# Taking GpSimd off SBUF in the first part of a two-layer block: its arithmetic moved to VectorE

## The chip, the cores and the metric

The kernel runs on one core of one Trainium2 chip. The core's engines are TensorE (PE: matrix products and transposes, results in PSUM), VectorE (DVE), ScalarE (ACT), GpSimd (POOL) and SyncE (SP, which here only issues DMA transfers). Each engine works through its own queue of instructions in order and waits on semaphores for the others. The metric is the time of one execution on the device in microseconds (us), the median of several executions; one execution more was recorded with a profile, and all rows below come from that one.

## The reference, cut to what matters

Two blocks follow each other on 256 tokens of width 2048, all in float32. The first is an RWKV-7 block and a feed-forward network, both modulated by a vector computed from a condition `c` (the ada projection, 2048 x 12288); the second is an attention and convolution block with a gated projection.

```
mod = silu(c) @ ada_w + ada_b                       # six vectors of 2048
h = rms(x) * (1 + sc_m) + sh_m
xx = token_shift(h) - h
r, k, v = (h + xx * mu[i]) @ w_rkv[i]               # three mixes, and three more for the low ranks
w, a, g = low-rank functions of further mixes
y = rwkv7_scan(r, decay, k, v, -kk, kk * a)         # 32 heads of 64, a recurrence over tokens
x = x + g_m * rms((groupnorm(y) + bonus) * g @ w_o)
h = rms(x) * (1 + sc_f) + sh_f
x = x + g_f * rms((silu(gate) * val) @ w_out)       # gate, val = conv(h @ w_in), hidden 5504
x = second_block(x)                                 # attention, short conv, w_out, gated projection
```

## The kernel before

Each matrix product is done in three passes: an operand is split into a high part (rounded, by ScalarE) and a low part (the remainder, by a subtraction), and TensorE adds high x high, high x low and low x high. Activations and weights are both split. For weights this is the helper `split` (line 133): a unit of 128 x 1024 is loaded into `raw`, ScalarE writes `whi` (line 143), and line 147 writes `wlo = raw - whi`. Which engine does that subtraction is a running count: with `share[0]` = n every n-th unit goes to GpSimd and the others to VectorE; `n_pool[0]`, set at the begin of some stages, sends the next few units to GpSimd.

The stages in order of time, with the letters by which the text calls them:

- **A**, the mixes and the k, v and low-rank products, in five groups of the 16 row tiles (`GROUPS`). `prep` and `mix` (line 366) make the mixed activations: VectorE writes `mt` (line 373), ScalarE the high part (line 376), and line 377 the low part, on VectorE for one mix of six and on GpSimd for the others.
- **B**, a loop over 16 pairs of heads. For each pair the low-rank products, decay, keys and the r product (two weight units) are made; GpSimd splits the low-rank weights (line 563), copies the last decay of each chunk into `EC` (line 588), and does the two multiplications of lines 593 and 603.
- **C**, the chunked scan over four chunks of 64 tokens. At its start (called the head here) VectorE inverts 32 x 32 triangles by a long row of small operations (`invert_diag`, lines 682 and 685), while `gram` (line 687) makes the Gram matrices: TensorE writes them to PSUM, ScalarE copies them to SBUF (line 705), and GpSimd multiplies the mask in (line 706); 16 of these 32 multiplications belong to the head. After it, line 806 multiplies the state by the decay on GpSimd.
- **D**, the output projection `w_o`, with `share[0]` = 3.
- **E**, the residual (`add_residual`, line 983), the second norm and the transposes into the feed-forward layout (`to_fm`; line 1002 scales, line 1022 writes low parts, two of eight on GpSimd).
- **F**, everything behind: the feed-forward network and the second block.

Through B, C, D and E, and again through F, runs the accumulation of the ada projection (`ada_group`, line 223) as a generator: each step loads two tiles of `ada_w` into a ring of buffers (three from B on) and adds them into an accumulator. `ada_pool[0]` = 1 sends one row tile of four to ScalarE (line 243, into `nbr`) and GpSimd (line 244), the other three are one VectorE instruction each (line 246); `ada_fm` then adds the two accumulators on GpSimd (line 279) before TensorE sums them over partitions.

A scheduler places the instructions on each engine's queue when the program is built, from the written order and its dependencies, so the written order shows only which work belongs together. DMA transfers are all issued from SP's queue.

## Time and profile before

| | |
|---|---|
| median of 3 executions | 2203.3 us (2195.14 to 2216.86) |
| the profiled execution, on the device | 2202.33 us |
| its span, first to last instruction | 2200.5 us |
| mean granted TensorE clock | 0.938 of full speed |
| busy: PE / DVE / ACT / POOL | 2007.2 / 1390.0 / 1025.5 / 770.4 us |
| DMA | 445.26 MB, mean 202 GB/s |

Times in the rows are microseconds from the span's start. An engine counts as busy while any of its instructions stands in the record. A timeline row gives start, duration, engine, source line, operation, what it writes and reads with the shapes, how many were merged, and in brackets the idle time of the engine before it with what ended it. Two VectorE instructions without a dependency overlap in the record by some 0.06 to 0.1 us, so a row of n merged ones lasts a little less than n times one.

### The profile page before, as it was taken

The page shows a single profiled execution, that of the slowest core. Times are in us where ns is not written, and L with a number is a line of the kernel's source. Part 1 is how long each engine was busy: PE and PEld are TensorE (multiplying, and loading weights), DVE is VectorE, ACT ScalarE, POOL GpSimd, SP SyncE. Part 2 cuts the span into 40 slices and gives each one's busy share as a digit, 9 for nine tenths or more (in the row PEclk, how much of TensorE's full clock was granted, in tenths as well). Part 3 has the DMA queues.
Part 4 walks back from the last instruction along what each step waited for, and adds up shares of the span by engine and source line. Part 5 has one row for each costly group of instructions (what it writes and reads, how often), then busy time and mean ns, then how long its engine had stood idle before and what let it go on. Part 6 is the DMA issues. An engine that isn't in the chain of part 4 may idle for free.

```text
span 2200.5 us, 36863 instructions
## 1 busy us (share of the span) xinstructions
PE 2007.2 (91%) x14708; PEld 1752.7 (80%) x14708; DVE 1390.0 (63%) x1975; ACT 1025.5 (47%) x1594; POOL 770.4 (35%) x437
## 2 busy tenths in 40 slices
PE   6889988987799696899999999999998999999998
PEld 3578777876577475789989999878886799998887
DVE  3576998987877767786666675433335565656435
ACT  3434455553344434555545545444435454454443
POOL 2332445656145334343333232222322222222232
PEclk9999998999679698899999999999999999999999
DMA  8778567774566687676676565665554444456554
GB/s 293 252 249 301 180 207 240 241 230 96 140 160 182 224 288 261 219 270 197 197 215 203 193 209 191 196 214 189 188 190 145 147 158 163 160 163 209 186 194 152
DMA packets 189037, 445.26 MB, mean 202 GB/s; under 512 B 40121, under 2 KB 62777, under 8 KB 187329
## 3 DMA queue, kind: packets, MB, share of 16 engines
q1 hardware_dynamic: 188864, 442.91, 62.4%
q8 instruction: 115, 1.88, 0.3%
q14 instruction: 58, 0.47, 0.1%
HBM read 427.10 MB, written 15.75 MB: 201 GB/s over the span
## 4 chain that ended last, share of the span: by engine, by line
PE 51%; DVE 5%; DMA 4%; ACT 1%; issue 1%; POOL 1%; SPq 0%; ACTq 0%; POOLq 0%; DVEq 0%
PE ps_s L158 6%; PE ps_s L160 6%; PE ps_s L159 5%; PE ps_s L175 4%; PE ps_s L174 4%; PE ps_s L173 4%; PE ps_g L158 4%; PE ps_g L160 4%; PE ps_g L159 4%; PE ps_g L173 3%; PE ps_g L175 3%; PE ps_g L174 3%; DMA raw<-in_ada_w 2%; DVE acc L246 1%; DVE wlo L147 1%
## 5 line engine op out<-in xcount | busy, mean ns | idle before, releaser
L143 ACT ACTIVATE whi<-raw 128x1024 fp32r<-128x1024 f32 x558 | 588.5, 1057 | 647.7 <-PE ps_s L174 126.5
L147 POOL TENSOR_TENSOR wlo<-raw,whi 128x1024 fp32r<-128x1024 f32 x185 | 458.1, 2477 | 984.6 <-ACT whi L143 950.0
L147 DVE TENSOR_TENSOR wlo<-raw,whi 128x1024 fp32r<-128x1024 f32 x373 | 480.3, 1290 | 439.5 <-ACT whi L143 435.2
L160 PE MATMUL ps_g<-xh,wlo 128*128 128x256 f32 x816 | 235.5, 289 | 7.6 <-DVE wlo L147 7.0
L160 PE MATMUL ps_s<-xh,wlo 128*128 128x256 f32 x816 | 230.7, 283 | 9.6 <-DVE wlo L147 9.3
L159 PE MATMUL ps_g<-xl,whi 128*128 128x256 f32 x816 | 235.0, 288 | 2.5 <-POOL xl L1022 2.5
L158 PE MATMUL ps_g<-xh,whi 128*128 128x256 f32 x816 | 235.8, 289 | 0.7 <-DVE kac L407 0.6
L158 PE MATMUL ps_s<-xh,whi 128*128 128x256 f32 x816 | 230.1, 282 | 2.6 <-ACT whi L143 2.6
L159 PE MATMUL ps_s<-xl,whi 128*128 128x256 f32 x816 | 229.6, 281 | 0.0
L246 DVE SCALAR_TENSOR_TENSOR acc<-raw,sil,acc 128x512 f32<-128x512 f32 x176 | 184.5, 1048 | 28.0 <-DMA raw<-in_ada_w 26.6
L160 PEld LDWEIGHTS ps_g<-xh,wlo 128*128 128x128 f32 x816 | 160.5, 197 | 10.4 <-DVE wlo L147 9.6
L160 PEld LDWEIGHTS ps_s<-xh,wlo 128*128 128x128 f32 x816 | 156.5, 192 | 11.4 <-DVE wlo L147 10.7
L159 PEld LDWEIGHTS ps_g<-xl,whi 128*128 128x128 f32 x816 | 161.7, 198 | 4.7 <-POOL xl L1022 2.7
L158 PEld LDWEIGHTS ps_g<-xh,whi 128*128 128x128 f32 x816 | 160.9, 197 | 4.4 <-ACT whi L143 1.3
L158 PEld LDWEIGHTS ps_s<-xh,whi 128*128 128x128 f32 x816 | 156.7, 192 | 3.0 <-ACT whi L143 3.0
L159 PEld LDWEIGHTS ps_s<-xl,whi 128*128 128x128 f32 x816 | 157.3, 193 | 0.0
L244 POOL TENSOR_TENSOR acc<-acc,nbr 128x512 f32<-128x512 f32 x48 | 75.5, 1572 | 140.6 <-ACT nbr L243 139.7
L158 PE MATMUL ps_s<-h3h,whi 128*128 128x256 f32 x384 | 109.6, 285 | 0.0
L160 PE MATMUL ps_s<-h3h,wlo 128*128 128x256 f32 x384 | 108.8, 283 | 0.0
L159 PE MATMUL ps_s<-h3l,whi 128*128 128x256 f32 x384 | 108.4, 282 | 0.0
L373 DVE SCALAR_TENSOR_TENSOR mt<-xx,vec,h 128x256 f32<-128x256 f32 x96 | 75.5, 828 | 6.9 <-POOL yl L377 4.7
L158 PEld LDWEIGHTS ps_s<-h3h,whi 128*128 128x128 f32 x384 | 72.5, 189 | 3.6 <-issue 3.5
(519 smaller groups left out, 4981.7 us busy)
## 6 DMA issues: line engine op xcount, KB each, us to landing
raw<-in_w_f SPq DMA_DIRECT2D x258, 512.0 KB, 4.4
raw<-in_ada_w SPq DMA_DIRECT2D x192, 512.0 KB, 5.2
raw<-in_w_i2f SPq DMA_DIRECT2D x80, 512.0 KB, 3.7
raw<-in_w_o SPq DMA_DIRECT2D x60, 512.0 KB, 4.7
raw<-in_w_v SPq DMA_DIRECT2D x32, 512.0 KB, 4.0
raw<-in_w_k SPq DMA_DIRECT2D x32, 512.0 KB, 4.3
raw<-in_w_r SPq DMA_DIRECT2D x32, 512.0 KB, 6.7
raw<-in_w_g SPq DMA_DIRECT2D x32, 512.0 KB, 4.7
```

The source lines that it names most:

```text
L143: S.activation(hi, raw, AF.Copy)
L147: e.tensor_sub(lo, raw, hi)
L158: mm(acc, wh[:, sl], xh[:, kt, :], start=(kt == 0), stop=False)
L159: mm(acc, wh[:, sl], xl[:, kt, :], start=False, stop=False)
L160: mm(acc, wl[:, sl], xh[:, kt, :], start=False, stop=(kt == KT - 1))
L173: mm(a, xh, wh[:, sl], start=st, stop=False)
L174: mm(a, xl, wh[:, sl], start=False, stop=False)
L175: mm(a, xh, wl[:, sl], start=False, stop=sp_)
L244: G.tensor_tensor(acc, acc, tp, op=ALU.add)
L246: V.scalar_tensor_tensor(acc, raw[:, a, :], sc, acc, op0=ALU.mult, op1=ALU.add)
L373: V.scalar_tensor_tensor(mt[:, i, :], xx[:, k0 + i, :], vcol(V_MU, m * 16 + k0 + i), hx[:, k0 + i, :], op0=ALU.mult, op1=ALU.add)
```

## The change

From the first stretch (A) to the output projection and the residual (E), every instruction with which GpSimd read SBUF moves to VectorE; what GpSimd keeps there are memsets and the four additions of squares at the very start (line 359). In parts:

- `split`: the low parts of all weight units of A, B and D on VectorE (`SH`, and 9999 instead of 3 for the output projection). `share[0]` = 3 comes back before F.
- `mix`: the low part always on VectorE. `to_fm`: likewise (`TFP` goes).
- B: lines 563, 593 and 603 on VectorE; the copy into `EC` becomes a second, small exponential on ScalarE, read from the same sums.
- `gram`: one VectorE instruction reads PSUM and multiplies the mask, in place of ScalarE's copy and GpSimd's multiplication.
- The state's decay (line 806) on VectorE.
- `ada_pool` stays 0: all row tiles of the ada projection are added by VectorE, and lines 238, 243, 244 and 279 no longer run, in F too.

```
-SH = (4, 3)
+SH = (9999, 9999)
...
-        (V if m == 1 else G).tensor_sub(dst[1][:, ks, :], mt, dst[0][:, ks, :])
+        V.tensor_sub(dst[1][:, ks, :], mt, dst[0][:, ks, :])
...
     ada_how[0] = ada_group
-    ada_pool[0] = 1
...
-        G.tensor_sub(l2l, l2, l2h)
+        V.tensor_sub(l2l, l2, l2h)
...
-        G.tensor_copy(EC[:, j, :], ep[:, :, 64])
+        S.activation(EC[:, j, :], c3(pc)[:, :, 63], AF.Exp, scale=C1)
...
-        G.tensor_tensor(k2, k2, kr, op=ALU.mult)
+        V.tensor_tensor(k2, k2, kr, op=ALU.mult)
...
-        G.tensor_tensor(bk[:, :, 64:128], c3(k2), em, op=ALU.mult)
+        V.tensor_tensor(bk[:, :, 64:128], c3(k2), em, op=ALU.mult)
...
-                S.activation(gg, gp[hd].rearrange("p (c t) -> p c t", t=P), AF.Copy)
-                G.tensor_tensor(gg, gg, gmask[:, None, :].broadcast_to([P, 4, P]), op=ALU.mult)
+                V.tensor_tensor(gg, gp[hd].rearrange("p (c t) -> p c t", t=P),
+                                gmask[:, None, :].broadcast_to([P, 4, P]), op=ALU.mult)
...
-                        G.tensor_tensor(s_, s_, ec, op=ALU.mult)
+                        V.tensor_tensor(s_, s_, ec, op=ALU.mult)
...
-    n_raw[0], share[0] = NRAW2, 3
+    n_raw[0], share[0] = NRAW2, 9999
...
-                e = G if k2 % TFP == 2 else V
-                e.tensor_sub(dst[1][:, ks, :], tf, dst[0][:, ks, :])
+                V.tensor_sub(dst[1][:, ks, :], tf, dst[0][:, ks, :])
...
     pho.close()
 
+    share[0] = 3
     n_pool[0] = NPL
```

The scheduler's order changes with it. Line numbers behind line 33 are one to seven lower after the change. In the loop over head pairs (B), VectorE's queue for one pair stood before as follows, from the evaluation of one pair (`qb`, line 610) to the next:

```order
L610 SCALAR_TENSOR_TENSOR qb<-ps_g,vec,k_3575 128x256
L240 TENSOR_SCALAR acc_3814<-raw,sil 128x512
L620 TENSOR_TENSOR vT<-vT,ps_m 128x256
L623 SCALAR_TENSOR_TENSOR vT<-vT,vec,ps_s 128x256
L246 SCALAR_TENSOR_TENSOR acc_3814<-raw,sil,acc_3814 128x512
L597 SCALAR_TENSOR_TENSOR kn<-kr,vec,ps_m 128x256
L582 SCALAR_TENSOR_TENSOR pc<-smask,thw 128x256
L246 SCALAR_TENSOR_TENSOR acc_3814<-raw,sil,acc_3814 128x512
L599 SCALAR_TENSOR_TENSOR AR<-kn,ep 128x4x64
L601 SCALAR_TENSOR_TENSOR pc<-tha,em 128x256
L602 SCALAR_TENSOR_TENSOR BK<-pc,kn 128x4x64
L607 TENSOR_TENSOR AR<-ps_g,ep 128x4x64
```

After the change the second half of the same place, up to the next pair's evaluation, reads:

```order
L146 TENSOR_TENSOR wlo<-raw,whi 128x1024
L597 SCALAR_TENSOR_TENSOR AR<-kn,ep 128x4x64
L599 SCALAR_TENSOR_TENSOR pc<-tha,em 128x256
L601 TENSOR_TENSOR BK<-k_3705,em 128x4x64
L600 SCALAR_TENSOR_TENSOR BK<-pc,kn 128x4x64
L239 TENSOR_SCALAR acc_3805<-raw,sil 128x512
L561 TENSOR_TENSOR l2l<-l_3812,l2h 128x512
L245 SCALAR_TENSOR_TENSOR acc_3805<-raw,sil,acc_3805 128x512
L146 TENSOR_TENSOR wlo<-raw,whi 128x1024
L605 TENSOR_TENSOR AR<-ps_g,ep 128x4x64
L608 SCALAR_TENSOR_TENSOR qb<-ps_g,vec,k_3705 128x256
```

The multiplication into `BK` (601), the low-rank low part (561) and the weight units' low parts (146) now stand in VectorE's queue ahead of the evaluation for which TensorE waits.

At the scan's head VectorE's queue began before with the masked diagonal blocks (659), a transpose, and at once the row of small operations of the inversion (682, 685):

```order
L623 SCALAR_TENSOR_TENSOR vT<-vT,vec,ps_s 128x256
L659 TENSOR_TENSOR TQ<-ps_s,cst 128x16x32 x2
L662 STREAM_TRANSPOSE NT<-TQ 128x1024
L670 COPY XT<-NT 128x1024
L682 TENSOR_TENSOR pt_5220<-XT,NT 128x30
L682 TENSOR_TENSOR pt_5241<-XT,NT 128x23
```

After the change the masks of the Gram matrices (703, from PSUM) stand between them:

```order
L621 SCALAR_TENSOR_TENSOR vT<-vT,vec,ps_s 128x256
L703 TENSOR_TENSOR xh<-ps_m,cst 128x4x128
L657 TENSOR_TENSOR TQ<-ps_s,cst 128x16x32 x2
L703 TENSOR_TENSOR xh<-ps_a,cst 128x4x128
L660 STREAM_TRANSPOSE NT<-TQ 128x1024
L703 TENSOR_TENSOR xh<-ps_m,cst 128x4x128
L668 COPY XT<-NT 128x1024
L703 TENSOR_TENSOR xh<-ps_m,cst 128x4x128
L680 TENSOR_TENSOR pt_5197<-XT,NT 128x30
```

Four of the 16 masks of the head stand here and twelve near the end of the first inversion; all 16 come before the transpose (725 before, 723 after) for which TensorE waits.

In the residual (E), VectorE's queue before, from the first root to the scaling by the second (1002):

```order
L338 RECIPROCAL rsy<-rsy 128x1
L983 SCALAR_TENSOR_TENSOR xt<-y_8004,rsy,xt 128x512 x2
L1051 TENSOR_TENSOR y_8004<-ps_s,grow 128x512
L983 SCALAR_TENSOR_TENSOR xt<-y_8004,rsy,xt 128x512 x2
L246 SCALAR_TENSOR_TENSOR acc_8644<-raw,sil,acc_8644 128x512
L975 TENSOR_REDUCE rsy<-ssq 128x1
L246 SCALAR_TENSOR_TENSOR acc_8644<-raw,sil,acc_8644 128x512 x2
L338 RECIPROCAL rsy<-rsy 128x1
L246 SCALAR_TENSOR_TENSOR acc_8644<-raw,sil,acc_8644 128x512
L983 SCALAR_TENSOR_TENSOR xt<-y_8004,rsy,xt 128x512 x4
L975 TENSOR_REDUCE rsx<-ssq_8553 128x1
L246 SCALAR_TENSOR_TENSOR acc_8644<-raw,sil,acc_8644 128x512
```

And after:

```order
L337 RECIPROCAL rsy<-rsy 128x1
L977 SCALAR_TENSOR_TENSOR xt<-y_7898,rsy,xt 128x512 x2
L1044 TENSOR_TENSOR y_7898<-ps_s,grow 128x512
L977 SCALAR_TENSOR_TENSOR xt<-y_7898,rsy,xt 128x512 x2
L969 TENSOR_REDUCE rsy<-ssq 128x1
L337 RECIPROCAL rsy<-rsy 128x1
L977 SCALAR_TENSOR_TENSOR xt<-y_7898,rsy,xt 128x512 x4
L969 TENSOR_REDUCE rsx<-ssq_8434 128x1
L337 RECIPROCAL rsx<-rsx 128x1
L996 TENSOR_SCALAR y_7898<-xt,rsx 128x512 x3
```

Five additions of the ada projection (246) stood inside this piece of the queue; after the change they stand ahead of it.

## Rows read from the trace of the kernel before

**Rows 1.** The page: the span, and part 1, busy us, share, instructions.

```profile
span 2200.5 us, 36863 instructions
PE 2007.2 (91%) x14708; PEld 1752.7 (80%) x14708; DVE 1390.0 (63%) x1975; ACT 1025.5 (47%) x1594; POOL 770.4 (35%) x437
```

**Rows 2.** Busy us by stretch (A, B, head, C, D, E): PE, PEld, DVE, ACT, POOL; clock, DMA.

```profile
35.00:325.00 290.00, 260.97 (x1680) 206.30 (x1678) 209.60 (x254) 133.57 (x172) 101.28 (x44) 0.97 0.71 239
325.00:505.00 180.00, 160.47 (x1146) 146.23 (x1146) 154.34 (x208) 96.39 (x188) 107.17 (x106) 0.91 0.72 226
505.00:565.00 60.00, 34.74 (x654) 27.65 (x643) 48.07 (x129) 18.08 (x36) 35.31 (x21) 0.80 0.42 98
565.00:725.00 160.00, 151.41 (x2145) 121.82 (x2142) 122.54 (x255) 75.34 (x169) 63.48 (x51) 0.78 0.65 171
725.00:860.00 135.00, 110.14 (x474) 84.32 (x471) 93.85 (x109) 56.23 (x83) 53.94 (x27) 0.84 0.75 262
860.00:910.00 50.00, 27.75 (x170) 25.21 (x169) 38.27 (x59) 24.35 (x51) 18.69 (x10) 0.73 0.63 221
```

**Rows 3.** TensorE's waits, one stretch each (A, B, head, D, E, E): us, times, longest.

```profile
PE ps_s L426 <- POOL wlo L147: 4.3, 1, 4.3
...
PE ps_m L612 <- DVE qb L610: 10.4, 5, 2.6
...
PE ps_m L735 <- DVE TQ L725: 15.9, 1, 15.9
...
PE ps_g L175 <- POOL wlo L147: 2.4, 2, 1.8
...
PE ps_m L1006 <- DVE y L1002: 17.9, 2, 17.0
PE ps_g L159 <- POOL xl L1022: 2.5, 1, 2.5
```

**Rows 4.** Timeline: VectorE instructions beside which GpSimd reads nothing.

```profile
143.86 2.45 DVE L373 SCALAR_TENSOR_TENSOR mt<-xx,vec,h 128x256 f32<-128x256 f32 x6
824.92 1.23 DVE L147 TENSOR_TENSOR wlo<-raw,whi 128x1024 fp32r<-128x1024 f32 x1 [4.19 <-ACT whi L143]
837.29 0.75 DVE L246 SCALAR_TENSOR_TENSOR acc<-raw,sil,acc 128x512 f32<-128x512 f32 x1 [0.73 <-DMA raw<-in_ada_w]
```

**Rows 5.** VectorE's groups of instructions in A (first row) and B: busy us, mean ns.

```profile
L373 DVE SCALAR_TENSOR_TENSOR mt<-xx,vec,h 128x256 f32<-128x256 f32 x92 | 72.8, 832 | 6.8 <-POOL yl L377 4.7 <-POOL xl L377 1.8
...
L246 DVE SCALAR_TENSOR_TENSOR acc<-raw,sil,acc 128x512 f32<-128x512 f32 x33 | 37.5, 1138 | 0.9 <-DMA raw<-in_ada_w 0.8
...
L602 DVE SCALAR_TENSOR_TENSOR BK<-pc,kn 128x256 f32<-128x256 f32 x16 | 20.0, 1248 | 0.3
```

**Rows 6.** Timeline of the scan's head: VectorE's inversion, and GpSimd's masks beside it.

```profile
516.97 1.29 DVE L659 TENSOR_TENSOR TQ<-ps_s,cst 128x512 f32<-128x512 f32 x2 [11.79 <-PE ps_s L655]
...
537.49 2.57 DVE L685 TENSOR_TENSOR XT<-XT,pt 128x91 f32<-128x91 f32 x2
...
549.82 0.35 DVE L682 TENSOR_TENSOR pt<-XT,NT 128x70 f32<-128x70 f32 x2
...
556.89 1.38 DVE L682 TENSOR_TENSOR pt<-XT,NT 128x23 f32<-128x23 f32 x2
...
561.86 1.99 DVE L725 STREAM_TRANSPOSE TQ<-XT 32x1024 f32<-32x1024 f32 x1
...
525.54 18.12 POOL L706 TENSOR_TENSOR xh<-xh,cst 128x512 f32<-128x512 f32 x6
```

**Rows 7.** Timeline of E: VectorE.

```profile
866.08 4.23 DVE L983 SCALAR_TENSOR_TENSOR xt<-y,rsy,xt 128x512 f32<-128x512 f32 x2
...
873.76 3.51 DVE L246 SCALAR_TENSOR_TENSOR acc<-raw,sil,acc 128x512 f32<-128x512 f32 x2
...
881.54 4.06 DVE L1002 TENSOR_SCALAR y<-xt,rsx 128x512 f32<-128x512 f32 x2
...
885.59 0.87 DVE L1002 TENSOR_SCALAR y<-xt,rsx 128x512 f32<-128x512 f32 x2
```

More of the change, by code (lines that the diff above doesn't have):

```diff
@@ L33 @@
 OSTEP = (2, 2, 2, 0)
-TFP = 8
 RSKIP = (0, 4)
@@ L896, in ada_steps @@
     def ada_steps(n):
-        ada_pool[0] = 4
         for _ in range(n):
             next(ada, None)
-        ada_pool[0] = 1
         yield
@@ L905, in body @@
         run(HD[nm]())
-    ada_pool[0] = 1
     dg = invert_diag(1, PARTS)
@@ L958, in body @@
             y_split(yh[1][:, :, p4, (c - 2) * 64:(c - 1) * 64], YS[c][:, p4, :])
-    ada_pool[0] = 1
     phb.close()
```

## The prediction, made before the run

> **What bounds the kernel now.** I read the page first: TensorE is busy for 91% of a span of 2200.5 us, VectorE for 63%, GpSimd for 35% [rows 1]. Such shares average stages with different limits, so the next view is the busy time by stretch [rows 2]. Up to 910 us, where the change acts, TensorE has gaps: 290.0 - 261.0 = 29.0 us in A, 180.0 - 160.5 = 19.5 in B, 25.3 in the head of the scan, 8.6 in the rest of C, 24.9 in D and 22.3 in E, together 130 us. No change to the vector engines can give back more than that, apart from the clock (granted share 0.73 to 0.97 in these stretches). Behind 910 us GpSimd keeps its third of the weight units, and I count that part as unchanged.
>
> Then the waits of TensorE, stretch by stretch [rows 3]. In A one wait of 4.3 us is for a low part made by GpSimd. In B it is for `qb` on VectorE, in the head 15.9 us in one piece for VectorE's transpose behind the inversion, in D partly for GpSimd's low parts, in E 17.9 us for VectorE's scaling and 2.5 for a low part of GpSimd. So in B, the head and E the engine that is waited for is VectorE, the one that gets the work.
>
> The last view is what VectorE's instructions last. With GpSimd not reading, a low part of a weight unit (128x1024) takes 1.23 us, an ada addition 0.75, and six mixes of 128x256 together 2.45, or 0.41 each [rows 4]; two masked blocks of 128x512, read from PSUM as the Gram matrices will be, take 1.29 [rows 6]. Yet the 92 mixes of A have a mean of 0.83 us, the 33 ada additions of B 1.14, and the 16 of line 602 there 1.25 [rows 5]. In the scan's head it is seen directly: a pair of small operations takes 2.57 us at 537.49 and 0.35 at 549.82, and in the first of these places GpSimd is in a run of six masks, 18.12 us or 3.02 each [rows 6]. Two engines that never wait for each other's data slow each other by whole instructions. The Trainium skill, "SBUF — State Buffer", section "Who interferes with whom", states this as an exclusive lock: a VectorE instruction with two inputs in SBUF and a GpSimd instruction that reads SBUF exclude each other. The trace agrees, with 2.57 against 0.35 us.
>
> **The change part by part.** The moved work, at these durations, less the roughly 0.1 us by which independent neighbours overlap.
>
> *A.* VectorE gets 18 weight low parts at 1.13 (20 us), 13 mixes' low parts of 128x1024 at 1.13 (15) and 13 of 128x512 at about 0.62 (8): 43 us. The excess that should leave is 92 x (0.83 - 0.41) = 39 us in the mixes alone [rows 4, 5], some more in the weight units. VectorE stays near 210 of 290 us. TensorE's gain is in single waits: in the one of 4.3 us, GpSimd made two low parts one after the other; on VectorE they take 1.2 each, about 2 us sooner. Counting one more such place: -4. Bounds: -15, if half of A's 29 us of gaps go; +5, if low parts that had an engine of their own queue behind mixes.
>
> *B.* VectorE gets 10 weight low parts (11 us), 12 ada additions (8), 16 low-rank low parts of 128x512 at 0.6 (10) and 32 multiplications of 128x256 at 0.36 (11): 40 us. It loses 33 x (1.14 - 0.75) = 13 us in the ada additions, 16 x (1.25 - 0.42) = 13 in line 602, and some of the remaining groups. It is busy for 154 of 180 us now, and so it will be after. The order shows the moved work in front of the evaluation that TensorE waits for; before, the same place was delayed by blocked instructions of up to 2.5 us. I take -2. Bounds: -10.4, the wait on `qb`; +14, if nothing of the excess comes back: 154 + 40 = 194, against 180. The exponential that replaces the copy into `EC`, 128x4, lies on ScalarE, idle for 84 us of B: nothing; without that cover its 16 would cost below 0.4 us each.
>
> *The head of C.* From 516.97 to 561.86 VectorE runs without a gap, 44.9 us [rows 6], and TensorE waits for what comes at the end. From 537.49 to 549.82 stand five rows at 2.5 us each where 0.4 would do: 12.3 - 2.0, some 10 us. One before them is slow too, and two shorter places, of which one row stands (1.38 us for 128x23), lose together some 6 by my estimate: 16.5. In their place come 16 masks of 128x512 from PSUM at 0.6, or 9.6 us, all ahead of the transpose. Net -7. Bounds: -14, if most masks fall into waits for TensorE; 0, if the shorter places have another cause and only the 10 us go. ScalarE's 32 copies of the Gram matrices go; it was idle there, so nothing.
>
> *The rest of C.* The other 16 masks (10 us), some 31 ada additions by the order (20) and 16 multiplications of the state (6) come, on 160 - 122.5 = 37.5 us of idle time. If half of that is paid by excess that goes, VectorE is busy for 140 of 160; TensorE is busy for 151, at a granted clock of 0.78. The waits for GpSimd's masks go, the queue gets fuller: 0, between -6 and +9.
>
> *D.* 11 low parts and about 17 additions come to VectorE (24 us), which is busy for 94 of 135, and a comparable excess goes. Low parts for which TensorE waited on GpSimd, 2.4 us in one group [rows 3], are made in 1.23 [rows 4]; against that the additions of the ada projection become one chain of 16 on VectorE, four more at 0.66 or 2.6 us longer, less the closing addition on GpSimd. SP's queue, in which ada tiles stand between those of `w_o`, waits for VectorE alone, no longer for ScalarE and GpSimd as well. -4, between -14 and +5.
>
> *E.* Everything is on one chain here. Two residual additions take 4.23 us where two of the ada addition's kind and size take 1.4, -2.8; two ada additions of 3.51 lie in front of the second root and, by the order, no longer do: -3.0, with half a microsecond left for ScalarE's root; two scalings take 4.06, against 0.87 for the same two elsewhere in E, -3.2 [rows 7]; a low part of 128x512 in 0.65 where TensorE waited 2.5 for GpSimd's, -1.8 [rows 3]. Together -10.8, so -11. Bounds -14, with further short excesses, and -5, if the ada additions moved ahead delay the chain's start.
>
> *F.* 16 ada additions (11 us) over 1290 us, with VectorE idle for nearly half: 0, between -3 and +4.
>
> **The sum** is -4 - 2 - 7 + 0 - 4 - 11 = -28 us. It is made against the profiled execution, 2202.3 us on the device (span 2200.5), which lies 1.0 below the median of the runs shown. So 2174 for an execution like it and **2175** beside the median.
>
> **The rivals.** One per cent, 22 us, is about what a measurement of this kernel can tell from no change.
>
> *More comes back.* The waits removed feed each other: buffers free earlier, weights land earlier, and TensorE, with shorter gaps, is granted the full clock for longer. The stretches around the head, C and D, have a mean of 0.78 to 0.84 of 2.4 GHz, that is, partly 1.2 GHz. With A -12, B -8, the head -10, C -4, D -12 and E -13 the sum is -59: 2144. For it speaks that all stretches lose contention at once; against it that VectorE's total does not fall. Chance 0.15.
>
> *Only E is shorter.* Low parts that came from two engines come from one queue; the short waits on GpSimd turn into waits on VectorE, which in A to D is as busy as before. Then A to D together give nothing, the head's -7 going back in a longer rest of C, and E -8: 2195. For it speaks that the order puts moved work ahead of `qb`; against it the single blocked instructions of 2.5 us, which a full but even queue does not have. Chance 0.25.
>
> *Slower.* VectorE becomes the bound in B and C. That needs the excess to stay: if the long instructions came from something other than GpSimd's reads, B would last 154 + 40 = 194 us instead of 180, and C (head and rest) would have 171 + 10 + 36 = 217 us of VectorE in 220, where 49 us of its idle time are waits for other engines; if half of these stay, 241, or 21 more. With nothing from A, D and E that is +35, 2238. It decides once less than half of the excess leaves. Against it stands the pair at 0.35 us, the same operation on hardly fewer elements, 12 us behind one of 2.57 [rows 6]. The Trainium skill, "Perfetto Trace Analysis", section "Identifying the Most-Contended Engine", would have the engine with the highest occupancy relieved, and in B that is, beside TensorE, VectorE with 86%; the change loads it further. By the bare counting of occupancy this rival follows. Chance 0.08.
>
> **How the numbers follow.** The forecast, 2157 to 2190, has 0.52. Of it, about 0.42 lies below 2181 (1% under the median). With the first rival, 0.15, that is 0.57 for faster; the second, 0.25, and the other 0.10 of the forecast give 0.35 for the same; the third 0.08 for slower. The range for 8 in 10 takes in half of the first rival and the second: 2145 to 2204.
>
> **What would show it.** Right, if in the profile after: VectorE's mixes in A have a mean near 0.45 us and its ada additions near 0.75, while its busy time by stretch stays within some 8 us; the inversion's pairs are all below 0.8 us and TensorE's wait behind it is nearer 9 than 16; the stretch from the last product of `w_o` to the transposes of the second norm is shorter by about 10. Wrong, if these instructions stay long with GpSimd silent; or if they become short and TensorE's waits on `wlo` and `qb` in A, B and D add up to more than before, which would be the second rival; or if the time behind E moves.

## The result, and the profile after

The changed kernel takes 2147.7 us, the median of 4 executions (2133.2 to 2150.2), beside 2207.2 for the kernel before on the same chip. The ratio, made from these and two more executions of the changed kernel (2140.2 and 2142.2 us), is 0.9714, with a 95% interval of 0.9663 to 0.9765; the two medians alone would give 0.973. The forecast was 2175, in a range of 2145 to 2204. The direction is right and the time lies in the range, but the gain of 59 us is twice the 28 of the sum. It is what the first rival gave (2144), which had a chance of 0.15.

The profiled execution of the changed kernel has a span of 2131.4 us, 69.1 below that of before. The page, to be read beside [rows 1] (the changed kernel's line numbers are 1 to 7 lower):

```profile
span 2131.4 us, 36666 instructions
PE 1979.3 (93%) x14708; PEld 1735.8 (81%) x14708; DVE 1385.3 (65%) x2203; ACT 972.3 (46%) x1514; POOL 386.8 (18%) x193
```

VectorE has 228 instructions more and is not busier. TensorE does the same 14708 products in 27.9 us less, at a granted clock of 0.945 instead of 0.938, and is idle for 152.1 us instead of 193.3. So 41 of the 69 us are gaps that closed. In the other 28 the same products took less time; the rise of the mean clock makes about 15 of them by my estimate (0.007 of 0.945, on 2007.2 us), and what makes the rest is not shown.

The busy time by stretch answers to [rows 2]. Each stretch begins with the TensorE instruction that began it before (A, B, head, rest of C, D, E, F); columns as there.

```profile
36.90:304.20 267.30, 254.78 (x1680) 204.71 (x1678) 204.59 (x294) 133.33 (x171) 0.14 (x2) 0.98 0.77 260
304.20:468.30 164.10, 154.58 (x1147) 140.63 (x1148) 148.91 (x279) 92.16 (x192) 5.21 (x18) 0.94 0.79 247
468.30:521.10 52.80, 42.17 (x661) 30.73 (x650) 38.60 (x135) 12.74 (x27) 2.06 (x3) 0.87 0.58 150
521.10:693.80 172.70, 142.37 (x2133) 119.14 (x2131) 135.91 (x316) 54.65 (x132) 3.59 (x2) 0.76 0.64 166
693.80:814.20 120.40, 103.44 (x478) 80.44 (x479) 95.70 (x141) 43.62 (x63) 0.00 (x0) 0.87 0.83 284
814.20:854.80 40.60, 25.10 (x169) 22.72 (x168) 35.75 (x57) 22.34 (x47) 10.84 (x4) 0.79 0.65 229
854.80:2131.40 1276.60, 1238.08 (x8376) 1128.75 (x8375) 712.73 (x959) 601.50 (x864) 358.75 (x152) 0.98 0.59 191
```

VectorE's busy time is 9 us lower in the head and 13 higher in the rest of C, and within 6 elsewhere. TensorE's waits in the first six stretches, one for each, answer to [rows 3]:

```profile
PE ps_s L446 <- DVE wlo L146: 1.1, 1, 1.1
...
PE ps_m L610 <- DVE qb L608: 0.3, 1, 0.3
...
PE ps_m L733 <- DVE TQ L723: 0.5, 1, 0.5
...
PE ps_a L733 <- DVE TQ L723: 11.4, 2, 10.0
...
PE ps_g L173 <- DVE xl L855: 5.9, 1, 5.9
...
PE ps_m L1000 <- DVE y L996: 15.5, 2, 14.5
```

The waits for weight low parts in A are down to two groups of 1.1 and 1.3 us, those for `qb` in B and behind the first inversion to half a microsecond or less. A new one of 10 us stands in the rest of C, behind the second inversion. VectorE's instructions, the mixes in A and two groups in B, answer to [rows 5]:

```profile
L372 DVE SCALAR_TENSOR_TENSOR mt<-xx,vec,h 128x256 f32<-128x256 f32 x90 | 39.5, 477 | 0.2
...
L245 DVE SCALAR_TENSOR_TENSOR acc<-raw,sil,acc 128x512 f32<-128x512 f32 x45 | 33.4, 743 | 0.1
...
L600 DVE SCALAR_TENSOR_TENSOR BK<-pc,kn 128x256 f32<-128x256 f32 x16 | 6.7, 417 | 0.0
```

0.48 us for 0.83, 0.74 for 1.14, 0.42 for 1.25: these are the durations of [rows 4], as forecast.

### The profile page after: what moved, and what is told of

Its sections match the earlier page's. It is cut to its first block, busy times and chain, and to the rows that moved or that the text cites. A ratio compares the mean times of both kernels' runs of the same rounds, so it can differ in the third digit from the quotient of the medians.

```text
span 2131.4 us, 36666 instructions
## 1 busy us (share of the span) xinstructions
PE 1979.3 (93%) x14708; PEld 1735.8 (81%) x14708; DVE 1385.3 (65%) x2203; ACT 972.3 (46%) x1514; POOL 386.8 (18%) x193
## 4 chain that ended last, share of the span: by engine, by line
PE 63%; DVE 8%; DMA 6%; issue 1%; ACT 1%; SPq 0%; POOL 0%; DVEq 0%; ACTq 0%; POOLq 0%
PE ps_s L157 6%; PE ps_s L159 6%; PE ps_s L158 6%; PE ps_g L159 4%; PE ps_g L157 4%; PE ps_g L158 4%; PE ps_g L174 4%; PE ps_g L172 4%; DMA raw<-in_ada_w 4%; PE ps_g L173 4%; PE ps_s L172 4%; PE ps_s L174 4%; PE ps_s L173 4%; DVE acc L245 2%; DVE wlo L146 1%
## 5 line engine op out<-in xcount | busy, mean ns | idle before, releaser
L146 DVE TENSOR_TENSOR wlo<-raw,whi 128x1024 fp32r<-128x1024 f32 x410 | 504.1, 1232 | 411.8 <-ACT whi L142 409.2
L146 POOL TENSOR_TENSOR wlo<-raw,whi 128x1024 fp32r<-128x1024 f32 x148 | 363.9, 2460 | 1085.7 <-ACT whi L142 1046.7
L245 DVE SCALAR_TENSOR_TENSOR acc<-raw,sil,acc 128x512 f32<-128x512 f32 x240 | 200.4, 836 | 35.3 <-DMA raw<-in_ada_w 33.6
L157 PE MATMUL ps_g<-h3h,whi 128*128 128x256 f32 x256 | 74.3, 290 | 0.0
```

Of the source, the lines that this page charges most:

```text
L146: e.tensor_sub(lo, raw, hi)
L157: mm(acc, wh[:, sl], xh[:, kt, :], start=(kt == 0), stop=False)
L245: V.scalar_tensor_tensor(acc, raw[:, a, :], sc, acc, op0=ALU.mult, op1=ALU.add)
```

## The experiments

Each kernel was compared with executions of the kernel before on its own chip, whose median went from 2207 to 2222 us from chip to chip, so ratios are compared. The table gives the length of the stretches in the profiled executions, in us, each from the start of the TensorE instruction that begins it to that of the next; F runs to the end of the span. A kernel called b_ is the kernel before with one edit, one called a_ or d_ the changed kernel with one or two.

| kernel | ratio (95% interval) | A | B | head | C | D | E | F |
|---|---|---|---|---|---|---|---|---|
| before | 1 | 289.5 | 179.8 | 60.0 | 160.0 | 135.1 | 50.0 | 1290 |
| b_ctl, the same | one time | 294.1 | 180.4 | 62.0 | 173.5 | 136.2 | 49.8 | 1298 |
| after | 0.971 (0.966 to 0.977) | 267.3 | 164.1 | 52.8 | 172.8 | 120.4 | 40.6 | 1277 |
| a_ctl, the same | one time | 268.7 | 169.9 | 53.6 | 176.8 | 122.8 | 40.1 | 1284 |
| b_mix | 0.990 (0.986 to 0.994) | 270.8 | 178.2 | 60.7 | 161.7 | 138.0 | 48.6 | 1295 |
| b_wlo | 0.987 (0.983 to 0.991) | 284.0 | 178.9 | 51.0 | 160.9 | 125.9 | 51.1 | 1294 |
| b_ada | 0.984 (0.982 to 0.987) | 294.8 | 171.9 | 61.5 | 147.7 | 130.2 | 47.4 | 1290 |
| b_gram | 0.986 (0.984 to 0.988) | 294.3 | 179.8 | 55.5 | 155.3 | 121.0 | 49.8 | 1287 |
| b_loc | 1.000 (0.997 to 1.003) | 292.4 | 182.8 | 54.5 | 175.3 | 135.7 | 48.3 | 1294 |
| b_mt3 | 1.001 (0.999 to 1.004) | 298.0 | 178.3 | 60.4 | 166.4 | 135.6 | 50.0 | 1295 |
| d_paced | 0.982 (0.977 to 0.987) | 281.8 | 171.7 | 46.1 | 175.7 | 122.7 | 41.7 | 1296 |
| a_pre | 0.967 (0.964 to 0.971) | 268.3 | 169.4 | 53.4 | 175.8 | 122.6 | 40.1 | 1278 |
| a_F | 0.955 (0.952 to 0.959) | 268.9 | 167.0 | 55.5 | 179.5 | 122.9 | 34.9 | 1253 |
| a_Flate | 0.962 (0.959 to 0.965) | 266.8 | 171.5 | 53.4 | 153.8 | 165.5 | 34.6 | 1256 |
| b_row | 0.982 (0.978 to 0.987) | 293.3 | 175.2 | 51.2 | 148.5 | 134.8 | 49.2 | 1273 |
| a_row | 0.952 (0.948 to 0.956) | 267.3 | 159.9 | 47.7 | 159.1 | 122.7 | 42.4 | 1265 |
| a_Frow | 0.943 (0.940 to 0.946) | 271.2 | 157.1 | 50.8 | 156.8 | 121.1 | 34.5 | 1255 |

**Both kernels once more, on one chip.** No edit.

> The kernel before, unchanged, profiled on the same chip as the three others of this comparison, to see how far the lengths of the stretches move from one chip and execution to the next. Expected: each stretch within 4 us of the first profile, the part behind the output projection within 8.

> The changed kernel, unchanged, on the same chip. If its gain of 14 us behind the output projection is one of the change and no scatter, that part is 10 to 18 us shorter here too than in the kernel before; if it is scatter, within 6 us of it. The rest of C is 10 to 16 us longer than in the kernel before, and VectorE stands there for ada tiles for 14 us or more.

Measured: 2231.7 and 2154.1 us, one execution each. The kernel before repeats to 5 us per stretch, and to 7 in F, but not in C, which took 173.5 instead of 160.0: TensorE was busy there for 166.9 us instead of 151.4, with the same products, so C hangs on the granted clock, 0.68 there instead of 0.78. The changed kernel repeats to 6, and to 7 in F. By the two pairs the change gives A -22 and -25, B -16 and -11, the head -7 and -8, C +13 and +3, D -15 and -13, E -9 and -10, F -14 and -14. Of the expectations, A and C of the kernel before fell outside their 4 us, and the rest of C, expected to be 10 to 16 us longer after the change, was 3 longer.

**One part of the change at a time.** The edits are those of the diff, each made alone in the kernel before: `V` for `G` in `mix` (b_mix); `SH = (9999, 9999)`, and 9999 for the output projection (b_wlo); no `ada_pool[0] = 1` or `4` (b_ada); the eviction fused with the mask (b_gram); the four edits in the loop of head pairs (b_loc).

> The kernel before with one part of the change: the mixes' low parts all on VectorE. GpSimd keeps the weight low parts, ada additions, masks and the rest, so of its 101 us in A some 45 stay. The two runs of one part each behind the inversion and on the ada projection moved A by less than 6 us, so the 22 us that A gave back in the changed kernel come from this part, from the weight low parts, or from both together only. Theory L (each us of GpSimd reads costs A in proportion): half of A's gain, -8 to -12, so about 0.995 of before. A theory T (GpSimd's reads cost nothing until VectorE has nothing to spare; two engines are both needed silent): A gives 3 us or less with this part alone.

> The kernel before with one part of the change: up to the output projection every weight low part on VectorE (1.23 us there, 2.46 on GpSimd), none on GpSimd; behind it every third goes to GpSimd as before. Theory L: the other half of A's gain (-8 to -12), B about -5, D a few us: 0.985 to 0.993 of before. Theory R (the gain is that a weight low part is ready sooner): all of A's 22 us and most of B's 16 come with this part alone, 0.980 of before or less. Theory T: A and B together 5 us or less.

> The kernel before with one part of the change: all additions of the ada projection on VectorE, none through ScalarE and GpSimd. GpSimd keeps its weight low parts, mixes' low parts, masks and small work. It removes 48 + 16 additions on GpSimd, some 98 us of reads, most of them in C to F, and puts 48 more of 0.75 us on VectorE. Theory L: a part of D's and E's gain, little in A and B, -5 to -15, 2192 to 2202. A theory S, in which the gain comes from the ada tiles' buffers being freed sooner, so that SP's queue moves on and the weights land earlier: D's -15 and the -14 seen behind 910 us come with this part alone, -25 or more, 2180.

> The kernel before with one part of the change: the Gram matrices are masked in VectorE's own eviction from PSUM, without ScalarE's copy and GpSimd's mask. Theory L: the head of the scan is shorter by 7 (the wait behind the inversion 9 or less instead of 15.9), and the second half of the masks costs the rest of C a few us at most: 2195 to 2202. Against it: the rest of C, 12.8 us longer in the changed kernel than before, is longer because of these masks; then the head's gain is given back and the time is 2203 to 2212.

> The kernel before with the last part of the change alone: in the loop of the head pairs the low-rank low parts, the copy into EC and the two multiplications leave GpSimd, which keeps its weight low parts and the ada additions there. B, 10 to 16 us shorter in the changed kernel, was 8 us shorter with the ada part alone and 1 to 2 with the mixes' or the weights' part. If what is left of B's gain comes from these instructions, for which TensorE waits through the evaluation of qb: B 4 to 8 us shorter, 0.996 to 0.998. If they only pay off together with the rest: B within 2 us, 0.999 to 1.001.

The mixes' low parts alone give all of A's gain, 19 to 23 us; the weight low parts give 5 to 10 there, though the mixes' mean is nearly the same in both, 0.65 and 0.69 us. No theory had that split, though the ratio of b_wlo, 0.987, lies in the range of its theory L. The held-up microseconds don't count alike; the nearest reason is that it matters which reads stand at the two places where TensorE waited longest (4.3 and 5.0 us). D is 14 us shorter with the masks alone, 9 with the weights, 5 with the ada part, and 15 with all, so the parts overlap: of TensorE's 7.6 us of waits there for the ada sums, 1.8 are left with the masks alone and none with the weights alone. The head is 4.5 us shorter with the masks, its wait for the transpose 0.9 instead of 15.9, so this part alone removes that wait. The length shows it less well: b_wlo, b_loc and b_row keep the masks on GpSimd and a wait of 14.4 to 16.1 us, and their heads last 51.0 to 54.5. C, which the rival of that run wanted longer, is shorter by some 5 at least, and the whole by 1.4%, more than either theory had. The ada part gave the total of theory S, 1.6%, but not its places: D is 5 us shorter, F is as before, and 8 come from B and 12 or more from C. In both TensorE's gaps are as long as before (21 and 7 us), and its products take less time, at a granted clock of 0.98 instead of 0.91 in B and 0.82 instead of 0.78 in C; what raised the clock is not shown. In B the part of the loop alone changes nothing (TensorE even waits 19.1 us for `qb`), as its second expectation had it; no part alone takes these waits below 11 us, and only the parts together remove them. The five gains add up to 5.4%, the change as a whole gave 2.9%.

**Useless reads, with nobody waiting for them.** In the changed kernel GpSimd gets a small copy as a trigger, and behind it reads or fills of which nothing is used: in d_read and d_set at every place where it worked before, in d_light and d_paced only at the mixes of A.

```
d_read, d_light:  G.tensor_copy(dz[:, 512:513], trig)
                  G.tensor_tensor(dz[:, :w], cst[:, 0:w], cst[:, 128:128 + w], op=ALU.subtract)
d_set:            G.memset(dz[:, :w], 0.0)   in place of the subtraction, two or three times
d_paced:          G.tensor_copy(dz[:, 0:1], trig)   then as d_light
```

> The changed kernel, and beside it useless work on GpSimd that nobody waits for: wherever GpSimd worked up to the output projection before the change (every third weight unit, the mixes, the low-rank parts, the masks, some ada additions), it subtracts two pieces of a constant tile into a scratch tile, 128x512 or 128x256, about as many microseconds as it was busy there before (some 330 us). Nothing of the kernel's own work is changed. Theory L (GpSimd's reads lengthen VectorE's instructions, and these delay TensorE): VectorE's 92 mixes in A go back from 0.4 to about 0.8 us, and since the moved work now comes on top, the time is that of the prediction's third rival or near it, 2200 to 2240. Theory R (the moved work is only made sooner on the faster engine and without a handover; the sharing of SBUF is beside the point): nothing in the kernel's own dependences changes, so 2148, within 10.

> As the run with useless reads, but GpSimd fills the scratch tile with zeros instead, two or three fills in place of one subtraction, so it is busy at the same places and reads no large tile there. Theory L, if it is the reading: VectorE's mixes stay near 0.4 us, and the time stays at 2148, within 10. If any access of GpSimd to SBUF, writes too, lengthens VectorE's instructions: mixes near 0.8 and 2200 to 2240 as with the reads. Theory R: 2148, within 10.

> The changed kernel with a light dose of useless reads on GpSimd: at each of the mixes whose low part GpSimd made before (27), one element of the mix is copied, and then a constant tile is subtracted from itself, 128x512, as many elements as that low part had. No weight, mask or ada place has any. That is about 55 us of GpSimd in A, some 20% of it, so its queue is empty again before the next mix and no buffer is kept. Nothing of the kernel's own work is changed. Theory L (the reads themselves hold VectorE up, and TensorE with it): VectorE's mixes have a mean of 0.55 to 0.7 us instead of 0.48, A is 8 to 18 us longer than in the changed kernel (275 to 286 instead of 267 to 269), the rest as there: 0.975 to 0.980 of before. Theory H (a read delays only through the kernel's own dependences and GpSimd's queue): A within 3 us of 268, 0.970.

> The changed kernel with the light dose of useless reads in its right places. In the run before, and in that with the heavy dose, the compiler's ordering had put the subtractions, which depended on nothing, at the front of GpSimd's queue, so they all ran in the first 70 us (or 370) and the copies that should have set their pace waited behind them. Here each copy writes into the tile that the subtraction behind it overwrites, so the order is copy, subtraction, copy. At each of the 27 mixes whose low part GpSimd made before, it subtracts one constant piece of 128x512 from another, or two, about as many us as that low part had. Theory L: VectorE's mixes have a mean of 0.55 to 0.7 us instead of 0.48, A is 8 to 18 us longer than in the changed kernel, 275 to 286: 0.975 to 0.980. Theory H: A within 3 us of 268, 0.970.

d_read came to 1.073 (1.070 to 1.076), d_set to 0.990 (0.987 to 0.994), d_light to 0.992 (0.989 to 0.995). By its ratio none of the three met the time of any of its theories, and the times tell little: the subtractions and fills, which depended on nothing, had been ordered to the front, GpSimd was busy without a break, and the copies waiting behind them kept the buffers, for which VectorE waited 60, 15 and 11 us. What does tell is the duration of VectorE's mixes, beside reads (first row) and beside fills (second):

```profile
L386 DVE SCALAR_TENSOR_TENSOR mt<-xx,vec,h 128x256 f32<-128x256 f32 x96 | 79.6, 863 | 59.9 <-POOL dz L122 59.6
```

```profile
L389 DVE SCALAR_TENSOR_TENSOR mt<-xx,vec,h 128x256 f32<-128x256 f32 x96 | 42.2, 477 | 15.5 <-POOL dz L122 14.9
```

Reads lengthen them and fills don't. (The Trainium skill, "SBUF — State Buffer", section "Who interferes with whom", says of a VectorE instruction with two SBUF inputs just that: it contends with a GpSimd instruction that reads SBUF, not with one that only writes it. These rows agree, 0.863 against 0.477 us.) In d_paced the reads stood in their places. Its groups in A, the mixes, GpSimd's subtractions and its copies of one element per partition, and the longest of TensorE's waits there:

```profile
L382 DVE SCALAR_TENSOR_TENSOR mt<-xx,vec,h 128x256 f32<-128x256 f32 x92 | 54.3, 626 | 0.5
...
L124 POOL TENSOR_TENSOR dz<-cst 128x512 f32<-128x512 f32 x38 | 60.1, 1580 | 3.0
L122 POOL COPY dz<-mt 128x1 f32<-128x1 f32 x25 | 20.5, 819 | 200.8 <-DVE mt L382 200.7
...
PE ps_s L458 <- DVE wlo L156: 4.9, 3, 2.8
```

A takes 281.8 us instead of 267.3 to 268.7, and the mixes 0.63 instead of 0.48: theory L, in its numbers for A. TensorE's gaps in A are 23.2 us instead of 12.5, and its waits for weight low parts, all made by VectorE, add up to 9.1 us instead of 2.4. The ratio, 0.982, is just above the 0.975 to 0.980 of theory L, with an interval from 0.977; F, which has no useless reads, is 12 to 19 us longer there for a reason that stays open. So reads of which no instruction needs the result give back 13 to 14 of the 22 to 25 us of A. B to E had no such test. Of the rest of A's gain nothing was shown; that low parts come out of GpSimd later (2.4 to 2.7 us against 1.2) would be the nearest reason.

**A third buffer for the mixes.** In the kernel before: `mt = t_(pa, [P, 4, T], "mt", bufs=3)`.

> The kernel before with three buffers instead of two for the mixes' values, which VectorE writes and GpSimd reads when it makes their low parts. Nothing else is changed: GpSimd reads as much as before. With the mixes' low parts on VectorE A was 19 us shorter, with the weight low parts there 5.5 us, though about the same number of VectorE's held-up microseconds left in both. Theory H (handover: VectorE's mixes wait until GpSimd, at 2.4 to 2.7 us a low part, has read the buffer, and the weight low parts of both engines queue behind that): VectorE's waits of 6.5 us for these buffers go, and A is 5 to 12 us shorter; 0.994 to 0.998 of before. Theory L (only the reading counts): A within 3 us of before.

A is 298.0 us, theory H falls. The place of the longest wait put down to VectorE, 5.0 us, shows why. First before, with that wait at the end, then with three buffers, VectorE and GpSimd:

```profile
148.57 2.56 DVE L373 SCALAR_TENSOR_TENSOR mt<-xx,vec,h 128x256 f32<-128x256 f32 x1 [1.66 <-POOL yl L377]
151.06 1.21 DVE L147 TENSOR_TENSOR wlo<-raw,whi 128x1024 fp32r<-128x1024 f32 x1
...
145.90 4.95 POOL L377 TENSOR_TENSOR yl<-mt,yh 128x1024 fp32r<-128x1024 f32 x2 [2.84 <-ACT yh L376]
...
PE ps_s L447 <- DVE wlo L147: 5.5, 2, 5.0
```

```profile
147.52 2.02 DVE L373 SCALAR_TENSOR_TENSOR mt<-xx,vec,h 128x256 f32<-128x256 f32 x1
149.46 3.37 DVE L147 TENSOR_TENSOR wlo<-raw,whi 128x1024 fp32r<-128x1024 f32 x1
...
146.59 5.15 POOL L377 TENSOR_TENSOR yl<-mt,yh 128x1024 fp32r<-128x1024 f32 x2 [2.85 <-ACT yh L376]
```

The wait for the buffer, 1.66 us, is gone, but now the weight low part behind it lasts 3.37 us instead of 1.21: it ends at 152.8, 1.1 us behind the end of GpSimd's second low part at 151.7. TensorE waits 4.6 us instead of 5.0. The wait is put down to VectorE, and at this place GpSimd makes it.

**GpSimd silent to the end.** In the changed kernel, without `share[0] = 3`, with `n_pool[0] = 0`, and the one multiplication of F on VectorE.

> The changed kernel, and GpSimd reads nothing behind the output projection either: all weight low parts there and one multiplication per unit on VectorE. VectorE is busy for 712 us of the 1277 there, of which some 90 are instructions held up by GpSimd; 148 low parts of 1.23 us come, 182 us. TensorE is idle for only 39 us there. Theory L: the held-up instructions become short, a few us of TensorE's waits for low parts go: 0.965 to 0.970 of before. Against it: low parts from one engine come in a queue of one, TensorE waits more: 0.973 to 0.980.

0.955: faster still, by more than theory L had. F has 148 low parts more on VectorE and is 24 to 31 us shorter; E 5 to 6. E shows it in one place, the changed kernel first, then a_F:

```profile
822.54 5.38 DVE L977 SCALAR_TENSOR_TENSOR xt<-y,rsy,xt 128x512 f32<-128x512 f32 x2
828.45 1.40 DVE L977 SCALAR_TENSOR_TENSOR xt<-y,rsy,xt 128x512 f32<-128x512 f32 x2
...
819.26 8.12 POOL L146 TENSOR_TENSOR wlo<-raw,whi 128x1024 fp32r<-128x1024 f32 x3 [186.88 <-ACT whi L142]
```

```profile
836.64 1.40 DVE L977 SCALAR_TENSOR_TENSOR xt<-y,rsy,xt 128x512 f32<-128x512 f32 x2
```

In the changed kernel GpSimd is already making F's first low parts, which `n_pool` gives it, while the residual additions of E run. They take 5.38 us until GpSimd stops at 827.4, and 1.40 in the next pair.

**Late ada tiles in C.** VectorE stands twice in the changed kernel's C for a tile of the ada projection; then the transposes behind the second inversion follow. Below, the timeline of VectorE and SP's store of a quarter of the gate row ahead of the first wait, then the busy time in a part of the first wait (columns as in the stretches):

```profile
572.42 0.75 DVE L245 SCALAR_TENSOR_TENSOR acc<-raw,sil,acc 128x512 f32<-128x512 f32 x1 [7.77 <-DMA raw<-in_ada_w]
...
608.79 0.75 DVE L245 SCALAR_TENSOR_TENSOR acc<-raw,sil,acc 128x512 f32<-128x512 f32 x1 [8.57 <-DMA raw<-in_ada_w]
...
610.70 1.95 DVE L723 STREAM_TRANSPOSE TQ<-XT 32x1024 f32<-32x1024 f32 x1
...
560.21 1.13 SPq L313 DMA_DIRECT2D gmd<-adav  x1
```

```profile
565.20:568.40 3.20, 1.29 (x29) 1.03 (x28) 0.00 (x0) 0.13 (x1) 1.71 (x1) 1.00 0.96 19
```

Three edits were tried on it: tiles requested one earlier (a_pre), the first two quarters of the scan without ada steps, on a_F (a_Flate), and the gate row, line 313, stored at once (a_row, on a_F as a_Frow, on the kernel before as b_row).

```
a_pre:    if q + 1 < KT // n: issue(q + 1)        ahead of the additions of tile q
a_Flate:  ASTEP = ((0,), (0,), (1,) * 12, (2, 2, 2, 2, 2, 2, 1, 1))
a_row:    - SP.dma_start(dst[0, k0 * P:(k0 + nk) * P].rearrange("(k p) -> p k", p=P), r)
          + PE.transpose(p_[0:KT, P:2 * P], grt, ident)      once, after the fourth group
          + S.activation(row, p_[0:KT, P:2 * P], AF.Copy)
          + SP.dma_start(dst[0].rearrange("(k p) -> k p", p=P), row)
```

> The changed kernel, with each ada tile of the scan and of what follows requested one tile earlier (the transfer of tile q+1 is put into SP's queue ahead of the additions of tile q; same three buffers). In the changed kernel's rest of C, VectorE stands twice at an ada addition, 7.8 and 8.6 us, until the tile has landed, and the steps of the second inversion behind it make TensorE wait 10 us once. If the 12.8 us that the rest of C is longer are these two waits: they shrink to 3 us or less and the ratio to before falls from 0.971 to 0.965 or 0.968. If the transfers are late because the 16 DMA engines are full at that place (share 0.99 while only 80 GB/s move): the waits stay, and the ratio stays at 0.971.

> The changed kernel with GpSimd silent behind the output projection too (0.955 of before in the run above), and the ada projection's steps taken out of the scan's first two quarters: 0, 0, 12 and 14 steps in the four quarters instead of 6, 6, 8 and 6. In the changed kernel the rest of C is 12.8 us longer because VectorE's queue stands twice at an ada addition whose tile lands late, behind transfers in small packets, with the second inversion behind it. If that is the cause: the waits for tiles in front of the second inversion go, TensorE's wait for its transpose is below 3 us instead of 11, the rest of C is 8 us shorter or more, D longer by at most 4; 0.950 to 0.953. If VectorE is simply full there: the steps come later, C is as long or D takes back what C gives, 0.955 to 0.960.

> The changed kernel, with the gate row of the ada projection stored at once: its 2048 numbers, until now four transfers of 512 pieces of 4 bytes, are turned with one transposition on TensorE and stored as 16 pieces of 512 bytes. In both kernels each of the four small transfers takes 8 to 10 us until it has landed, with the DMA engines busy for over 0.9 while 10 to 20 GB/s move; in the changed kernel the two tiles for which VectorE stands in the rest of C, 9.6 and 9.8 us, were requested right behind two of them. Theory D (these transfers make the tiles late): the two waits fall to 3 us or less each, the rest of C is 155 to 165 us instead of 173 to 177, and the time 0.962 to 0.967 of before instead of 0.971. Theory O (the queue is too full, or the tiles are late for another reason, such as SP's queue or the norm's loads in pieces of 256 bytes): the waits stay at 14 us or more in all, and the ratio at 0.970.

> The same edit on the changed kernel with GpSimd silent behind the output projection too, which was at 0.955. Theory D: 0.946 to 0.951, the fastest of all. Theory O: 0.955.

> The same edit on the kernel before. There VectorE stands for ada tiles for 4 to 7 us in the rest of C, and reaches the additions behind these transfers later, since the masks and low parts of GpSimd hold it up. If the late tiles are a bound that only the change uncovers: 0.996 to 1.001. If they cost the kernel before as much: 0.990 or less.

Asking earlier did nothing for C, 175.8 us, with 19.8 of waits for tiles; the interval of its ratio reaches that of the changed kernel. Without the ada steps C is 26 us shorter than in a_F, but D, to which they move, is 43 longer, and the ratio 0.962 instead of 0.955: the second expectation, and a little worse. D has one long wait for the ada sums:

```profile
PE ps_m L280 <- DVE acc L245: 18.6, 2, 16.9
```

The stores of the row were the cause of the late tiles. Line 313 stores 512 numbers as 512 pieces of 4 bytes; the time from issue to landing in the changed kernel, then in a_row, and VectorE's waits for tiles in a_row's C:

```profile
DMA to landing us min/median/max: 8.3/9.8/10.6
```

```profile
DMA to landing us min/median/max: 1.4/3.4/5.5
```

```profile
DVE acc L245 <- DMA raw<-in_ada_w: 2.6, 2, 2.2
```

The waits fall from 16.3 us to 2.6, C to 159.1: theory D, with a ratio of 0.952 below its 0.962 to 0.967, as F and B are shorter too. SP's queue, which theory O named, had stood only 1.2 and 1.0 us for the numbers to be stored at these two places. (The Trainium skill, "DMA: Bandwidth & Descriptors", section "Why small descriptors are slow (HBM only)", has a fixed overhead of about three cycles per packet. That small pieces cost, the trace confirms; but by an estimate from the figures of that page 512 packets on 16 engines would take well under 1 us, and the measured 9.8 us for 2 KB decides. What makes the rest no run here shows.) But b_row gains nearly as much, 1.8% beside 2.0%, so its first expectation is wrong: the stores are no bound that the change uncovers. Both kernels pay for them, in C and, for the second row, in F. With these stores gone in both, C is still longer after the change, 159.1 us against 148.5, and there VectorE is busy for 136 us instead of 123, while TensorE's products take about as long (142.8 and 141.8 us). By this one pair that is what the moved work costs in C.

a_Frow, at 0.943 the fastest of all and below the 0.946 to 0.951 of its theory D, beats the changed kernel by 2.9%.

## Why the prediction was right in kind, and where it was mis-sized

The direction and the mechanism were right: VectorE's instructions became as short as they are without GpSimd's reads, except in E, its busy time over the span hardly moved, the pairs of the inversion last 0.52 us or less, and most of the waits on VectorE went. The sizes were not: the sum had -28 us, the stretches of the two pairs give -70 and -78. The step that failed is the price of TensorE's gain, which I took from single waits as the trace puts them down to an engine, with no term for the clock. One sign of being wrong came true, the time behind E moved; and VectorE's busy time did not stay within 8 us everywhere (-9 in the head, +13 in the rest of C). The sizes, term by term:

- **A, -4; measured -22 and -25, outside the bounds.** The step that failed is "TensorE's gain is in single waits": I counted the wait that the trace put down to GpSimd, halved, and one more place. But the waits put down to VectorE's weight low parts, 9.2 us in all, were GpSimd's as well: they are 2.4 after the change and 9.1 in d_paced, where GpSimd makes nothing and only reads, and b_mt3 shows it at one place. TensorE's gaps in A fell from 29.1 to 12.5 us. Another 5.7 came from products that took less time, at a granted clock of 0.98 instead of 0.97 (in the second pair 9.9, 0.98 instead of 0.95), which had no term.
- **B, -2; measured -16 and -11.** I held the wait for `qb`, 10.4 us, to be replaced by the moved work in front of it. It went to nearly nothing, with VectorE busy for 149 us, near the 154 that I had forecast. TensorE's gaps are 10 and 6 us less, the rest is products that took less time at a clock of 0.94 instead of 0.91 and 0.92. The bound I had set at -10.4 is the size it has in the second pair.
- **The head, -7; measured -7 and -8.** The sum was right by luck. TensorE's wait behind the inversion fell by 15.4 us, to 0.5 rather than 9, so I had priced it at half. What hides the other half is that 8 more of the 32 products of 128x512 in line 869 (before and after, below) now stand in the head and no longer in C, 7.5 us more. The 8.6 us in which TensorE waits for nothing that the profile shows were there before too, 9.0.

```profile
L871 PE MATMUL ps_g<-raw,ys 128*128 128x512 f32 x16 | 7.3, 599 | 0.0
```

```profile
L869 PE MATMUL ps_g<-raw,ys 128*128 128x512 f32 x24 | 14.8, 784 | 0.0
```

- **The rest of C, 0 (-6 to +9); measured +13 and +3.** The idle time of VectorE that I let the moved work fill was not free: the queue got fuller by 13 us, and the wait for late tiles in it grew from 4.2 and 7.4 to 16.3 and 19.4 us. TensorE's gaps grew from 8.6 to 30.3 us (6.6 to 31.7 in the second pair); the lengths show less of it, because C lost those eight products to the head and, in the second pair, its clock before was only 0.68. Its lengths before, 160.0 and 173.5, say that this term could be known to 13 us at best.
- **D, -4; measured -15 and -13.** The bound was -14. I had counted 2.4 us of waits on GpSimd's weight low parts and the ada sums as a loss; but TensorE waited 7.6 us for those sums, which GpSimd added, and 1.4 after the change. Its gaps are 8 us less in both pairs. The rest is products that took less time, at a clock of 0.87 instead of 0.84 in the first pair.
- **E, -11; measured -9 and -10.** Right as a sum and wrong in one term: the first two residual additions did not get shorter (5.38 us, 4.23 before), since GpSimd's first low parts of F fell on them; without these, in a_F, E is another 5 to 6 us shorter. TensorE's gaps are 7 us less, and 2 to 3 came from the clock (0.79 instead of 0.73), which had no term, so that the sum fits is in part luck.
- **F, 0; measured -14 in both pairs, outside the bounds.** The cause stays open. TensorE's gaps are 7 and 5 us less, and the same 8376 products took 6 and 9 us less, at a granted clock of 0.98 throughout. The ada part alone gives 1290 us, as before. And in d_paced, with the same instructions in F at the same clock, the products take 1258 us instead of 1238, and F 1296.

Of the rivals, "more comes back", with a chance of 0.15, is what happened by its number, its sizes within 14 us for A, B, the head, D and E, with C on the other side. Its mechanism, waits that feed each other and a higher clock, is shown only for the clock; A's waits went because GpSimd had made them. "Only E is shorter" fell with A and B. "Slower" needed most of the long instructions to stay, and outside E none did; relieving the busiest vector engine was not what counted, since VectorE after the change does more in the same time.

## What to carry to other kernels

Where two engines exclude each other, a wait that the trace puts down to the one may be made by the other: price the excess of the instructions in front of each wait, whatever engine is named. Give the granted clock a term of its own: in A, B and D it rose where gaps closed, and in b_ada where they did not. Work moved onto an engine's idle time is free only where nothing later in its queue is waited for. And look for transfers in pieces of a few bytes: a store of 2 KB took some 10 us to land, and made tiles of 512 KB behind it late.

## What had not been expected of the hardware

A transfer of 2 KB in 512 pieces of 4 bytes took 8.3 to 10.6 us to land, and in a stretch of it the DMA engines were busy for 0.96 while 19 GB/s moved. GpSimd waits as well: beside VectorE's mixes its copy of one element per partition took 0.82 us on the mean, when a copy could be done in 0.18 (the shortest seen in d_light). And with the rows of single numbers stored at once, a stretch in the middle of F runs at a granted clock of 1.00, 2.4 GHz, with TensorE hardly idle, whether GpSimd reads there or not: 282.7 us in b_row, where GpSimd is busy for 86.8, and 289.1 in a_Frow, where it is silent. With GpSimd silent and the old stores, a_F, it takes 294.4. Below are b_row, a_Frow and a_F (columns as in the stretches):

```profile
1178.80:1461.50 282.70, 282.58 (x2104) 266.93 (x2104) 161.30 (x200) 141.35 (x186) 86.77 (x37) 1.00 0.63 212
```

```profile
1103.10:1392.20 289.10, 289.10 (x2105) 273.64 (x2104) 182.60 (x237) 139.60 (x184) 0.00 (x0) 1.00 0.61 207
```

```profile
1135.20:1429.60 294.40, 286.68 (x2104) 269.73 (x2103) 182.71 (x238) 139.94 (x183) 0.00 (x0) 0.98 0.64 203
```
